# The opening of a one-core encoder layer: keys summed in PSUM in one written order, and a table of delays for the side steps

## The chip, the cores and the metric

The kernel runs on one core of a Trainium2 chip. The metric is the device time of one execution in microseconds (us). Before the change it is 957.74 us, the median of three runs (956.77 to 959.01). About 0.2%, some 2 us, is what a measurement of this kernel can tell from no change.

## The reference, cut to what matters

One transformer-like layer is computed for 512 prompt tokens and 32 sample tokens, together 544 columns. Everything behind it needs `h`, and `h` needs the layer norm of `x` and a shift and a scale that are columns of a matrix product with `w_ada`:

```python
mod = jnp.einsum('bd,de->be', jax.nn.silu(c), w_ada) + b_ada
sh1, sc1, g1, sh2, sc2, g2 = jnp.split(mod[:, None, :], 6, axis=-1)
h = layer_norm(x) * (1 + sc1) + sh1
z = jnp.einsum('btd,de->bte', h, w_in)
a_q, a_k, a_v, m_qk, m_v, m_if, m_o = jnp.split(z, IN_SPLITS, axis=-1)
```

`h` has 1024 features. The first 512 columns of `w_in` give the queries of four attention heads, the next 512 the keys, the next 512 the values. Attention, an mLSTM recurrence with a causal convolution ahead of it, gates, an output projection, two layer norms and a SwiGLU network follow.

## The kernel before

**Arithmetic.** Data are float32. A matmul on TensorE takes the float32r parts of both operands: a tensor is cut into `hi` (a rounded copy, made by ScalarE) and `lo` (the rest, by a subtraction on VectorE or GpSimd), and each product is three matmuls, hi by hi, hi by lo and lo by hi. `h` lies transposed, as eight tiles of 128 features by 544 columns, in `hH` and `hL` (a and b hold tiles 0 to 3 and 4 to 7). The columns are done in two halves, 256 and 288 (`HALF`).

**The stream.** Nearly all work is a list of `Unit`s, run by `stream` (line 678). A unit holds 128 output columns of a weight matrix: for each half it takes a PSUM bank, runs its tiles `k` with three matmuls each (line 604), and evacuates the bank. The weights come through a ring of two 1 MB buffers (`raw_tile`, loaded on SP's queue); the next unit's weights are split while one runs. PSUM has eight banks under four tags: three `g`, two `s`, two `x`, one `o`.

**Side steps.** Transposes, norms, softmax, the recurrence and the outputs are generators. `Lane` (line 34) keeps a reckoned clock while the program is written: `add` queues a generator with a due time, and `run`, called behind each tile `k` of a unit, steps what is due; the due time of the next step is the time so far plus what the generator yields, or the reckoned end of its last instruction (`chain`). So the lane fixes the order of instructions on each engine, not their times. `until` steps everything forward up to a condition. One long generator, `side_all`, holds attention, then four mLSTM heads, then the sample's; it must be through (`need_mn`) before the first unit of `w_br_b`.

**The opening.** The loads go out in order: rows of `x`, and the `w_ada` and `w_in` pieces of five stages of 1, 1, 2, 2 and 2 feature tiles (`STAGES`). For a stage, `ada_gemv` (line 437) makes the shift and scale columns with 32 small matmuls, `ada_first` (line 450) copies them out (`gs`), turns them with transposes (`gt`), reduces and adds the bias (`red`, `modT`), and `modulate` (line 420) makes tiles of `hH` and `hL`. `ORDER0` is a string with one letter for each step of the beginning: transposes of `x`, stage 0, and the first half of its keys and queries (line 507). All else of the queries and keys are units of one stage, one kind and one head, of only one or two tiles `k`. Their partial sums leave PSUM after each stage and are added to `qk` in SBUF by `qk_evac` (line 839): ScalarE writes in stage 0, ScalarE and GpSimd (`qk_t`) or VectorE (line 176) add in the later ones. Every unit takes one `g` bank for each half. `group_split` splits weights with ScalarE and GpSimd (line 157). `start_ada` begins the next stage during the units of one.

**Behind it.** `k_out` (line 866) turns the keys (`k_tok`) and stores them; `q_split` splits the queries. Then come the value units, the gates, convolution units, and so on in the same stream.

Of the kernel before, what the change touches and what calls it, by code (L numbers as in the profile page):

```python
# [32 lines left out]

class Lane:
# [6 lines left out]
    def __init__(self):  # L41
        self.t = 0.0
        self.chain = 0.0
        self.free = {"act": 0.0, "dve": 0.0, "pool": 0.0}
        self.q = []

# [16 lines left out]

    def add(self, gen, delay=0.0):
        item = [max(self.t + delay, self.chain), gen, False]
# [28 lines left out]
def trunk_kernel(ctx: ExitStack, tc: tile.TileContext, I: dict, O: list):  # L94
# [121 lines left out]
    ADA_AT = (0, 0)  # L216
    WARM = 0
    STAGES = (1, 1, 2, 2, 2)
    START = tuple(sum(STAGES[:i]) for i in range(len(STAGES)))
    ada_raw, w_raw = {}, {}  # L220

    def load_ada(s, dst):
        w = STAGES[s] * 128
        if not isinstance(dst, list):
            dst = [dst[:, 8 * i * w:8 * (i + 1) * w] for i in range(2)]
        ada_raw[s] = [d[:, 0:8 * w].rearrange("p (k c) -> p k c", k=8) for d in dst]
        for i in range(2):
            c0 = 1024 * i + START[s] * 128
            load(ada_raw[s][i], w_ada[:, c0:c0 + w].rearrange("(k p) c -> p k c", p=128))

    def load_w(s, dst):
        n = STAGES[s]
        w_raw[s] = dst[:, 0:1024 * n].rearrange("p (i k c) -> p i k c", i=2, k=n)
        for i, c0 in enumerate((512, 0)):
            r0 = START[s] * 128
            load(w_raw[s][:, i], w_in[r0:r0 + n * 128, c0:c0 + 512].rearrange("(k p) c -> p k c", p=128))
# [4 lines left out]
    s2a = [slot(f"2{c}", [128, 2176], F32, f"s2_a{c}") for c in "ab"]  # L241
    s3a = [slot(f"3{c}", [128, 2176], F32, f"s3_a{c}") for c in "ab"]
    s8a = slot(8, [128, 2048], F32, "s8_a")
# [10 lines left out]
    load_ada(0, raw_tile())  # L254
    load_w(0, raw_tile())
# [3 lines left out]
    load_ada(1, s8a)  # L259
    load_w(1, s7a[:, 3072:4096])  # L260
    load_ada(2, s2a)
    load_w(2, s7a[:, 1024:3072])
    load_ada(3, s3a)

# [81 lines left out]
    ORDER0 = "0p0c1c1wwg0gg21grgr2ghrhhh3hr2r3hr3hrammh"  # L346

# [16 lines left out]

    warm = bank("o", "warm")

    def keep_warm(n):
        for _ in range(n):
            tr(warm[:, 0:128], ident, 128)
# [50 lines left out]
    def modulate(k, part=None):  # L420
# [10 lines left out]
        (vtt if part != 0 else gtt)(hL(k)[:, c], t[:, c], hH(k)[:, c].bitcast(F32), SUB)  # L431

    def all_of(gen):
        for _ in gen:
            pass

    def ada_gemv(s):
        n = STAGES[s]
        w = n * 128
        ga = bank("o" if s % 2 else "x", "ga")  # L440
        for i in range(2):
            for k in range(8):
                g = 32 * (k % 4)
                nc.tensor.matmul(
                    ga[g:g + 32, i * w:(i + 1) * w], scT[:, k, :], ada_raw[s][i][:, k, :], start=(k < 4), stop=(k >= 4)
                )
                lane.pe(0.06 * n)
        return ga

    def ada_first(s, ga=None, part=None):  # L450
        n = STAGES[s]
        w = n * 128
        if ga is None:
            ga = ada_gemv(s)
        yield 0
        gs = tmp([128, 512], "gs")
        vcopy(gs[:, 0:2 * w], ga[:, 0:2 * w])
        yield 0
# [3 lines left out]
        yield 0  # L462
# [3 lines left out]
            in_=gt[:, 0:2 * w].rearrange("p (e g c) -> p e c g", g=4, c=32)[:, :, 0:2, :],  # L466
        )
        m = modT[:, 0:16, :].rearrange("p (i k) r -> p i k r", i=2)[:, :, START[s]:START[s] + n, :]
        b = PT[:, c_b_ada:c_b_ada + 16].rearrange("p (i k) -> p i k", i=2)[:, :, START[s]:START[s] + n]
        for i in range(2):  # L470
            vtt(
                m[:, i], red[:, i * n:(i + 1) * n, :], b[:, i].unsqueeze(2).to_broadcast([128, n, 2]), ADD
            )
        yield 0
        ms = [modulate(START[s] + k, part) for k in range(n)]
        for g in ms:
            next(g)
        yield 0
        for g in ms:
            all_of(g)  # L480

    groups = [(s, i) for s in range(len(STAGES)) for i in range(2)]
    parts = {}

    def group_split(x):
        if x in parts or x >= len(groups):
            return
        s, i = groups[x]
        n = STAGES[s]
        r = w_raw[s][:, i]  # L490
        hi = wp.tile([128, 2, 512], F32R, tag="hi", name="hi", bufs=2)
        lo = wp.tile([128, 2, 512], F32R, tag="lo", name="lo", bufs=2)
        act(hi[:, 0:n], r, AF.Copy)
        gtt(lo[:, 0:n], r, hi[:, 0:n].bitcast(F32), SUB)
        parts[x] = (hi, lo)
# [4 lines left out]
    def first_half():  # L500
        for x in range(2):
            hi, lo = parts[x]
            for h in range(4):
                ps = bank("g", "g")
                c = slice(128 * h, 128 * h + 128)
                for p, (w, a) in enumerate(((hi, hH), (hi, hL), (lo, hH))):
                    nc.tensor.matmul(ps[:, 0:256], w[:, 0, c], a(0)[:, 0:256], start=(p == 0), stop=(p == 2))
                act(qk_holder["kq"[x]][:, h, 0:256], ps[:, 0:256], AF.Copy, scale=0.125 if x else 1.0)
                yield

    xg = [x_tile(tt) for tt in range(4)] + [x_rows()]
    pc = silu_c()
    g0 = None
    m1 = None
    fh = first_half()

    def step(c):
        nonlocal g0, m1, ga1
        if c in "0123":
            next(xg[int(c)], None)  # L520
        elif c == "r":
            next(xg[4], None)
        elif c == "c":
            next(pc, None)
        elif c == "g":
            if g0 is None:
                g0 = ada_first(0, ada_gemv(0), 0)
            next(g0, None)
        elif c == "w":
            group_split(len(parts))  # L530
        elif c == "h":
            next(fh, None)
        elif c == "m":
            if m1 is None:
                m1 = modulate(0, 1)
            next(m1, None)
        elif c == "a":
            ga1 = ada_gemv(1)
        elif c == "p":
            load_params(prm_b)  # L540

    ga1 = None
    for c in ORDER0:
        step(c)
    params(prmB, 64)
    load_w(3, raw_tile())
    load_ada(4, slot(6, [128, 4096], F32, "s6_a"))
    load_w(4, raw_tile())
# [17 lines left out]

    def split_w(raw, nk, c0, eng=None):
        r = raw.rearrange("p (k c) -> p k c", c=256)
        hi = wp.tile([128, 8, 128], F32R, tag="hi", name="hi", bufs=2)
        lo = wp.tile([128, 8, 128], F32R, tag="lo", name="lo", bufs=2)  # L570
        act(hi[:, :nk], r[:, :nk, c0:c0 + 128], AF.Copy)
        (eng or vtt)(lo[:, :nk], r[:, :nk, c0:c0 + 128], hi[:, :nk].bitcast(F32), SUB)
        return hi, lo
# [265 lines left out]
    def qk_evac(s, i, h):  # L839
        def f(ps, hf, o, n):  # L840
            dst = qk_holder["kq"[i]][:, h, o:o + n]
            sc = 0.125 if i else 1.0
            if s == 0:
                act(dst, ps[:, 0:n], AF.Copy, scale=sc)
            elif s == 1 and hf:
                t = tmp([128, 288], "qk_t")
                act(t, ps[:, 0:n], AF.Copy, scale=sc)
                gtt(dst, dst, t, ADD)
            else:
                stt(dst, ps[:, 0:n], sc, dst, MUL, ADD)  # L850
                if hf and s == len(STAGES) - 1:
                    if i:
                        q_tasks.append(lane.add(q_split(h)))
                    else:
                        lane.add(k_out(h), 0.5)
# [637 lines left out]
    def stage_part(x, j):  # L1493
        def f():
            group_split(x)
            if j == 1:
                group_split(x + 1)
            c = slice(j * 128, (j + 1) * 128)
            return tuple(t[:, :, c] for t in parts[x])
        return f  # L1500

    fin = {}

    def start_ada(s):
        return lambda: fin.update({s: lane.add(ada_first(s))})

    lane.free = dict.fromkeys(lane.free, lane.t)
    lane.chain = lane.t
    fin[1] = lane.add(ada_first(1, ga1))

    def need_h(s):
        return lambda: lane.until(lambda: fin[s][2])

    for x, (s, i) in enumerate(groups):
        for h in range(4):
            u = Unit(
                None, 0, STAGES[s], hH, hL, qk_evac(s, i, h), ak0=START[s], split=stage_part(x, h),
                halves=(0, 1) if s else (1,),
            )
            if i + h == 0 and s:  # L1520
# [585 lines left out]
```

## Time and profile before

| what | us |
|---|---|
| median of three runs | 957.74 |
| the profiled execution | 960.61 |
| its span, first to last instruction | 958.9 |
| TensorE busy | 915.3 |
| VectorE busy | 524.9 |
| ScalarE busy | 353.5 |
| GpSimd busy | 201.7 |

The profiled execution is 1.7 us longer than its span and 2.9 us above the median. A TensorE row's duration overlaps that of its neighbours, since matmuls are pipelined: the pace is read from the distance of two starts. The granted clock (PEclk) says which share of full speed TensorE was given.

### The profile page before, as it was taken

To read this page: it belongs to the slowest core of one execution; us is meant where nothing else is said; L and a number is where in the kernel's file an instruction comes from. 1 tells how busy PE (TensorE), PEld (TensorE's weight loads), DVE (VectorE), ACT (ScalarE), POOL (GpSimd) and SP (SyncE) were. 2 spreads that over 40 slices of the span, in tenths; PEclk is the share of its full clock that TensorE was granted. 3 is DMA by queue.
4 is the path that set the end of the run, shared out by engine and by line. 5 is a ranking of instruction groups with operands and counts; after the bars stand their busy time and mean duration, and the time that the engine had idled before them with its cause. 6 is when DMAs were issued, how large, how long until landed. Compare 5 with 4: busy or idle time off the path is not lost. (4 is left out here: it accounts for less than half of the span.)

```text
span 958.9 us, 17324 instructions
## 1 busy us (share of the span) xinstructions
PE 915.3 (95%) x7184; PEld 866.9 (90%) x7184; DVE 524.9 (55%) x1124; ACT 353.5 (37%) x686; POOL 201.7 (21%) x241
## 2 busy tenths in 40 slices
PE   5799999999999999999999999999999999999995
PEld 4679998798798989889999989999999999999995
DVE  4657567877554454446855786544444443133257
ACT  4511466455542322322443564322222222122241
POOL 4433016332411110100651665300000000000001
PEclk9989999999999999999999999999999999999998
DMA  9904423252234234242931512022222224532302
GB/s 283 339 2 131 143 67 113 89 175 90 89 116 161 94 118 158 88 139 94 310 97 45 176 50 89 1 89 89 89 89 89 88 89 165 169 101 79 121 2 93
DMA packets 92282, 110.43 MB, mean 115 GB/s; under 512 B 3896, under 2 KB 75660, under 8 KB 92204
## 3 DMA queue, kind: packets, MB, share of 16 engines
q1 hardware_dynamic: 91996, 109.27, 35.2%
q8 instruction: 56, 0.92, 0.4%
q14 instruction: 22, 0.18, 0.1%
q10 hardware_dynamic: 208, 0.07, 0.0%
HBM read 102.09 MB, written 7.24 MB: 114 GB/s over the span
## 5 line engine op out<-in xcount | busy, mean ns | idle before, releaser
L153 DVE TENSOR_TENSOR lo<-raw,hi 128x1024 fp32r<-128x1024 f32 (+3 forms) x102 | 112.0, 1098 | 129.9 <-ACT hi L132 128.6
L132 ACT ACTIVATE hi<-raw 128x1024 fp32r<-128x1024 f32 (+2 forms) x124 | 122.1, 984 | 151.4 <-PE dn L604 61.7
L604 PE MATMUL dn<-act,hi 128*128 128x288 f32 (+1 forms) x704 | 134.8, 290 | 0.0
L604 PE MATMUL g<-hHa,hi 128*128 128x288 f32 (+1 forms) x344 | 109.2, 317 | 6.2 <-DVE qka L176 4.7
L604 PEld LDWEIGHTS dn<-act,hi 128*128 128x128 f32 x704 | 110.0, 188 | 0.0
L604 PE MATMUL g<-hHb,hi 128*128 128x256 f32 (+1 forms) x352 | 107.7, 306 | 1.3 <-DVE qka L176 1.3
L604 PE MATMUL g<-h2Ha,lo 128*128 128x288 f32 (+1 forms) x352 | 101.4, 288 | 2.4 <-POOL lo L157 1.5
L604 PE MATMUL g<-h2La,hi 128*128 128x288 f32 (+1 forms) x352 | 101.4, 288 | 1.0 <-DVE h2La L153 1.0
L604 PE MATMUL g<-h2Ha,hi 128*128 128x288 f32 (+1 forms) x352 | 102.1, 290 | 0.0
L604 PE MATMUL g<-hLa,hi 128*128 128x288 f32 (+1 forms) x344 | 101.2, 294 | 0.7 <-DVE hLa L153 0.6
L604 PE MATMUL g<-hLb,hi 128*128 128x256 f32 (+1 forms) x352 | 101.8, 289 | 0.0
L604 PE MATMUL g<-h2Hb,hi 128*128 128x288 f32 (+1 forms) x352 | 101.7, 289 | 0.0
L604 PE MATMUL g<-h2Lb,hi 128*128 128x288 f32 (+1 forms) x352 | 101.5, 288 | 0.1
L604 PE MATMUL g<-hHb,lo 128*128 128x256 f32 (+1 forms) x352 | 101.5, 288 | 0.0
L604 PE MATMUL dn<-act,lo 128*128 128x288 f32 (+1 forms) x352 | 101.1, 287 | 0.0
L604 PE MATMUL g<-hHa,lo 128*128 128x288 f32 (+1 forms) x344 | 100.9, 293 | 0.2 <-DVE lo L153 0.2
L604 PE MATMUL g<-h2Hb,lo 128*128 128x288 f32 (+1 forms) x352 | 100.9, 287 | 0.0
L157 POOL TENSOR_TENSOR lo<-raw,hi 128x1024 fp32r<-128x1024 f32 (+2 forms) x30 | 63.7, 2123 | 136.5 <-ACT hi L132 126.0
L604 PEld LDWEIGHTS g<-hHa,hi 128*128 128x128 f32 x344 | 66.3, 193 | 23.0 <-issue 6.2
L604 PEld LDWEIGHTS g<-hHb,hi 128*128 128x128 f32 x352 | 66.8, 190 | 5.3 <-issue 2.7
L157 POOL TENSOR_TENSOR rs__10439<-rs__10439,nhalf 128x1 f32<-128x1 f32 x1 | 1.0, 1047 | 325.2 <-DVE rs__10442 L147 325.2
L604 PEld LDWEIGHTS g<-h2Ha,lo 128*128 128x128 f32 x352 | 66.3, 188 | 3.2 <-POOL lo L157 2.0
(480 smaller groups left out, 2163.6 us busy)
## 6 DMA issues: line engine op xcount, KB each, us to landing
raw<-in_w_gu_dram SPq DMA_DIRECT2D x18, 1024.0 KB, 5.1
raw<-in_w_ada_dram SPq DMA_DIRECT2D x16, 1024.0 KB, 5.0
raw<-in_w_in_dram SPq DMA_DIRECT2D x10, 1024.0 KB
raw<-in_w_gate_dram SPq DMA_DIRECT2D x8, 1024.0 KB, 6.7
raw<-in_w_down_dram SPq DMA_DIRECT2D x8, 1024.0 KB, 5.2
wo<-in_w_o_dram SPq DMA_DIRECT2D x4, 1024.0 KB
rawg<-in_w_gu_dram SPq DMA_DIRECT2D x4, 1024.0 KB
raw<-in_w_down_dram SPq DMA_DIRECT2D x3, 768.0 KB
```

The source lines that it names most:

```text
L132: nc.scalar.activation(out=out, in_=in_, func=func, **kw)
L153: nc.vector.tensor_tensor(out=out, in0=in0, in1=in1, op=op)
L157: nc.gpsimd.tensor_tensor(out=out, in0=in0, in1=in1, op=op)
L604: nc.tensor.matmul(ps[:, 0:n], w[:, self.k0 + k, :], a(self.ak0 + k)[:, o:o + n], start=(self.first and k == 0 and p == 0), stop=(self.las ...
```

## The change

- **Stages.** The five stages keep their 1, 1, 2, 2 and 2 tiles. Each loads its `w_ada` columns and only the key half of its rows of `w_in`, one 0.25 MB load for a tile; all go out at the start, into buffers of their own. The first 256 query columns follow as the last load of the opening.
- **Sums in PSUM.** The keys of all four heads are summed over the eight tiles without leaving PSUM: the first halves of four heads in two `g` banks, the second halves in a `g`, two `s` and the `o` bank. ScalarE copies them out once (`e0`, `e1`).
- **One order.** `ORDER` lists all steps up to the keys: `x` for a step of `x`, `g` and `t` for a stage's columns and their turning, `m`, `a`, `b` for the steps of `modulate`, `w` for a split, `A`, `B` for the twelve matmuls of a tile in a half, `q` for the first query split. The `lo` parts of weights and of `h` are made by VectorE, none by GpSimd.
- **Queries.** They are four ordinary units of eight tiles, evacuated by ScalarE.
- **The table.** `LATER` has 114 entries: a name of a generator, which one of its kind, and which step. `Lane.add` and `Lane._step` add the entry, from -3 to 5.4 us, to the reckoned due time. Names of `norm_pair` (22), `attention.block` (21) and `side_all` (33) are the most. In `side_all` the entries for steps 155 to 219 sum to +6.8 us.

```diff
+    def later(self, item):
+        item[4] += 1
+        return LATER.get(f"{item[3]}/{item[4]}", 0.0)
...
-            item[0] = max(self.t + d, self.chain)
+            item[0] = max(self.t + d, self.chain) + self.later(item)
...
+    STAGES = ((0,), (1,), (2, 3), (4, 5), (6, 7))
...
+    ada_at += [slot(i, [128, 2048], F32, f"s{i}_a") for i in ("2a", "2b", "3a", "3b", 8, "5a")]
+    def load_stage(s):
+        load_ada(s, ada_at[2 * s:2 * s + 2])
+        for t in STAGES[s]:
+            load_w(t, w_k[:, t, :])
...
+    def k_split(s):
...
+        act(hi, w_raw[s], AF.Copy)
+        vtt(lo, w_raw[s], hi.bitcast(F32), SUB)
...
+    def acc_open(hf):
+        if hf == 0:
+            for i in range(2):
+                b = bank("g", "k_acc")
+                for j in range(2):
+                    acc[2 * i + j, 0] = b[:, 256 * j:256 * j + 256]
+        else:
+            for h, tag in enumerate("gsso"):
+                acc[h, 1] = bank(tag, "k_acc")[:, 0:288]
...
+        for p in passes:
+            w, a = ((hi, hH), (lo, hH), (hi, hL))[p]
+            nc.tensor.matmul(
+                acc[h, hf], w[:, c], a(s)[:, o:o + n],
...
+    ORDER = (
+        "x1 x0 p c x1 c x0 g0 w0 x2 x1 x2 x4 x0 x4 x3 x4 x2 t0 x4 x4 P a0 x3 g1 o0 t1 a0 x4 x3 A0 x4 b1 b0 o1 b0 a1 b1 a1 g2 w1 B0 t2 A1 m2 m3 B1 m3 w2 m2 g3 w3 B2 A2 t3 m5 B3 A3 m4 w4 m4 m5 g4 w5 B4 t4 m7 m6 m7 A4 m6 A5 w6 B5 A6 B6 w7 A7 q e0 B7 e1"
+    )
...
+            for h in range(NH):
+                act(qk_holder["k"][:, h, HALF[n][0]:sum(HALF[n])], acc[h, n], AF.Copy)
...
+            act(qk_holder["q"][:, h, o:o + n], ps[:, 0:n], AF.Copy, scale=0.125)
...
+    for h in range(NH):
+        lane.add(k_out(h), 1.0 + 2.0 * h)
+    for c in range(2):
+        units += hunits(w_in, c * 256, [q_evac(2 * c), q_evac(2 * c + 1)])
```

More of the change, by code (lines that the diff above doesn't have):

```diff
@@ L45, in __init__ @@
         self.q = []
+        self.count = {}
     def op(self, eng, out, k=1.0):
@@ L258, in trunk_kernel @@
     load_x(3)
[L259 to L263, printed above, removed]
+    for s in range(1, len(STAGES)):
+        load_stage(s)
     make_identity(nc, ident)
@@ L430, in modulate @@
         yield 0
[L431 to L435, printed above, removed]
+        vtt(hL(k)[:, c], t[:, c], hH(k)[:, c].bitcast(F32), SUB)
     def ada_gemv(s):
-        n = STAGES[s]
-        w = n * 128
-        ga = bank("o" if s % 2 else "x", "ga")
+        w = 128 * len(STAGES[s])
+        ga = bank("x", "ga")
         for i in range(2):
@@ L465, in ada_first @@
             out=red[:, 0:2 * n, :], axis=AX.X, op=ADD,
-            in_=gt[:, 0:2 * w].rearrange("p (e g c) -> p e c g", g=4, c=32)[:, :, 0:2, :],
+            in_=gt[:, 0:256 * n].rearrange("p (e g c) -> p e c g", g=4, c=32)[:, :, 0:2, :],
         )
[L468 to L495, printed above, removed]
+        lane.op("dve", red)
@@ L497, in trunk_kernel @@
     qk_holder = {}
     qk_holder["q"], qk_holder["k"] = Halves(5, F32, "qk").h
[L500 to L509, printed above, removed]
+    acc = {}
@@ new lines, in k_mms, with split_w @@
+    def k_mms(s, halves, passes):
+        for hf in halves:
+            for h in range(NH):
+                k_mm(s, h, hf, passes)
+    def split_w(raw, nk, c0, eng=None):
+        r = raw.rearrange("p (k c) -> p k c", c=256)
+        hi = wp.tile([128, 8, 128], F32R, tag="hi", name="hi", bufs=2)
+        lo = wp.tile([128, 8, 128], F32R, tag="lo", name="lo", bufs=2)
+        act(hi[:, :nk], r[:, :nk, c0:c0 + 128], AF.Copy)
+        (eng or vtt)(lo[:, :nk], r[:, :nk, c0:c0 + 128], hi[:, :nk].bitcast(F32), SUB)
+        return hi, lo
@@ L542, in trunk_kernel @@
-    ga1 = None
-    for c in ORDER0:
+        what, n = c[0], int(c[1:] or 0)
+        if what == "x":
+            next(xg[n], None)
+        elif what == "c":
+            next(pc, None)
+        elif what == "p":
+            load_params(prm_b)
+        elif what == "P":
+            params(prmB, 64)
+        elif what == "w":
+            k_split(n)
+        elif what == "g":
+            sums[n] = ada_gemv(n)
+        elif what == "t":
+            ada_turn(n, sums[n])
+        elif what in "mab":
+            part = {"m": None, "a": 0, "b": 1}[what]
+            if (what, n) not in mods:
+                mods[what, n] = modulate(n, part)
+            next(mods[what, n], None)
+        elif what == "o":
+            acc_open(n)
+        elif what in "AB":
+            k_mms(n, ("AB".index(what),), (0, 1, 2))
+        elif what == "e":
+            for h in range(NH):
+                act(qk_holder["k"][:, h, HALF[n][0]:sum(HALF[n])], acc[h, n], AF.Copy)
+        elif what == "q":
+            q_first.append(split_w(q_raw, 8, 0))
@@ L837, in setup, with q_evac @@
             yield 0
-    def qk_evac(s, i, h):
+    def q_evac(h):
         def f(ps, hf, o, n):
[L841 to L855, printed above, removed]
+            act(qk_holder["q"][:, h, o:o + n], ps[:, 0:n], AF.Copy, scale=0.125)
+            if hf:
+                q_tasks.append(lane.add(q_split(h)))
         return f
@@ L1491, in trunk_kernel @@
     SIDE_AT = 3
[L1493 to L1505, printed above, removed]
     lane.free = dict.fromkeys(lane.free, lane.t)
     lane.chain = lane.t
[L1509 to L1520, printed above, removed]
-                u.need = need_h(s)
-            units.append(u)
-            if (i, h) == ADA_AT and 0 < s and s + 1 < len(STAGES):
-                units.append(Call(start_ada(s + 1)))
+    for h in range(NH):
+        lane.add(k_out(h), 1.0 + 2.0 * h)
+    for c in range(2):
+        units += hunits(w_in, c * 256, [q_evac(2 * c), q_evac(2 * c + 1)])
+    q_chunk = units[0].chunk
+    q_chunk.emit = lambda: setattr(q_chunk, 'raw', q_raw)
+    units[0].split = lambda: q_first[0]
     units.append(Call(lambda: lane.add(setup())))
@@ L1537, in trunk_kernel @@
     units += vq
-    vch = [u.chunk for u in units if u.chunk]
-    vch[0].gate = lambda: 7 in parts
-    vch[-1].gate = lambda: 9 in parts
     units.append(IfUnit())
```

225 lines of the change are left out of this document (154 added, 71 removed).

## The prediction

> **What bounds the kernel now.** I read the busy shares first, then busy time by stage, then TensorE's waits, then the order of time at the opening.
>
> ```profile
> span 958.9 us, 17324 instructions
> PE 915.3 (95%) x7184; PEld 866.9 (90%) x7184; DVE 524.9 (55%) x1124; ACT 353.5 (37%) x686; POOL 201.7 (21%) x241
> 0.00:97.60 97.60, 77.65 (x621) 68.80 (x621) 59.92 (x139) 32.86 (x61) 39.24 (x54) 0.93 0.59 186
> 97.60:300.00 202.40, 196.23 (x1531) 176.30 (x1530) 133.75 (x331) 107.53 (x268) 59.30 (x72) 0.99 0.36 113
> 300.00:480.00 180.00, 180.00 (x1391) 164.41 (x1391) 99.74 (x274) 55.56 (x103) 31.32 (x49) 1.00 0.44 146
> 480.00:600.00 120.00, 113.75 (x889) 110.40 (x888) 82.40 (x148) 56.69 (x94) 59.92 (x58) 1.00 0.27 90
> 900.00:959.00 59.00, 47.67 (x377) 47.02 (x375) 33.52 (x60) 16.78 (x25) 4.22 (x4) 0.93 0.19 69
> ```
>
> TensorE is the bound: busy 915.3 of 958.9 us. The stage rows give, in this order, length, then busy time of TensorE, its weight loads, VectorE, ScalarE and GpSimd, then granted clock, DMA share and GB/s. Of 43.6 us of idle TensorE, 20.0 lie in the first 97.6 us, 6.2 in the next stage, 6.3 between 480 and 600, 11.3 at the end. I cut at 97.60 us because there the first value matmul starts (its row stands below), a work item that both kernels have; what lies behind it is a stream that moves forward as a whole if it starts earlier.
>
> In the opening, three more views say what holds it: what the DMA engines moved, TensorE's waits, and the granted clock after a wait.
>
> ```profile
> 0.00:10.00 10.00, 0.34 (x1) 0.18 (x1) 3.23 (x9) 2.83 (x4) 4.34 (x17) 1.00 0.79 239
> 10.00:20.00 10.00, 7.90 (x59) 6.49 (x60) 6.16 (x18) 5.37 (x9) 4.94 (x8) 0.97 1.02 300
> 20.00:30.00 10.00, 10.00 (x95) 9.42 (x93) 5.04 (x18) 7.35 (x20) 2.13 (x5) 0.86 1.08 359
> 30.00:40.00 10.00, 8.42 (x67) 6.54 (x66) 4.51 (x9) 3.84 (x11) 4.82 (x5) 0.83 1.08 359
> PE g L604 <- DVE qka L176: 6.0, 3, 3.5
> PE g L604 <- ACT qka L132: 1.5, 1, 1.5
> 45.38 0.40 PE L604 MATMUL g<-hHa,hi 128*128 128x288 f32 x1 [3.48 <-DVE qka L176]
> 45.00:50.00 5.00, 4.03 (x18) 3.39 (x19) 3.34 (x6) 2.75 (x6) 3.94 (x4) 0.66 0.32 114
> 50.00:55.00 5.00, 5.00 (x45) 3.25 (x44) 1.00 (x3) 0.00 (x0) 1.71 (x1) 0.65 0.00 0
> 55.00:60.00 5.00, 4.99 (x40) 4.79 (x40) 4.12 (x14) 1.90 (x3) 0.00 (x0) 1.00 0.00 0
> ```
>
> The DMA engines are full (share about 1) from 10 to 40 us. TensorE's waits of 6.0 and 1.5 us are for `qka`: a `g` bank whose partial sum had not been added to SBUF yet. After the longest, 3.48 us up to 45.38, the clock was 0.66 and 0.65 for about 10 us. So the opening is held by its data up to about 40 us, and then by evacuations and the clock that they cost.
>
> **Part 1: when the keys are done.** The change doesn't alter the key matmuls, it alters when they can run. By bytes, up to the last key tile there are 2.10 MB of `x`, 0.13 of sample rows, 8.39 of `w_ada` columns and 2.10 of key weights. The query half, 2.10 MB, now comes behind. Stage 3's `w_ada` columns end at 9.57 MB. The rates above sum to 2.39, 5.39 and 8.98 MB at 10, 20 and 30 us, so 9.57 MB have moved at 30 + 0.59/0.359 = 31.6 us, and stage 4's columns (12.19 MB) at 38.9.
>
> A landing is seen by its user somewhat later. The stage-0 query weights end at 2.62 MB, moved at 10.8 us by the same sum, and their split waited for them until 13.26, 2.4 us. So stage 3 is usable at 34.0 and stage 4 at 41.3.
>
> ```profile
> 13.26 0.63 ACT L132 ACTIVATE hi<-raw 128x512 fp32r<-128x512 f32 x1 [1.41 <-DMA raw<-in_w_in_dram]
> 68.80 1.93 PE L444 MATMUL ga<-s_a,scT 128*32 128x256 f32 x32
> 72.28 0.60 PE L142 MATMUL gt<-ident,gs 128*128 128x128 f32 x4
> 72.63 0.37 PE L604 MATMUL g<-hHb,hi 128*128 128x256 f32 x1
> 72.92 0.19 DVE L464 TENSOR_REDUCE red<-gt 128x8 f32<-128x32 f32 x1 [0.34 <-PE gt L142]
> 73.14 0.24 DVE L153 TENSOR_TENSOR modT<-red,PT 128x4 f32<-128x4 f32 x2
> 73.63 1.42 DVE L149 TENSOR_SCALAR mod_t<-xTb,modT 128x512 f32<-128x512 f32 x4
> 61.39 2.67 DVE L153 TENSOR_TENSOR hLb<-mod_t,hHb 128x544 fp32r<-128x544 f32 x2
> L153 DVE TENSOR_TENSOR anb<-qka,ana x4: 681/684/685, 95.2 to 101.1; 128x512 fp32r<-128x512 f32 x4
> 97.60 0.28 PE L604 MATMUL g<-hHa,hi 128*128 128x256 f32 x1
> 100.90 0.29 PE L604 MATMUL g<-hHa,hi 128*128 128x288 f32 x1
> 104.09 0.28 PE L604 MATMUL g<-hHa,hi 128*128 128x256 f32 x1
> 88.03 0.71 PE L142 MATMUL k_tok<-ident,qkb 128*128 128x128 f32 x5
> 88.49 0.38 PE L604 MATMUL g<-hHb,hi 128*128 128x288 f32 x1
> ```
>
> Steps of the written order, at full clock: a stage's 32 column matmuls 1.93 us; its four transposes 0.35 (72.28 to 72.63); the twelve matmuls of a tile in a half. A 288-column half of eight tiles took 3.19 us (100.90 to 104.09), that is 24 matmuls, so twelve take 1.59. The 256-column half took 3.30 from 97.60; 256/288 of 3.19 is 2.84, and the rest is a short wait, so twelve take 1.42.
>
> From 34.0 the order has g3, B2, A2, t3, B3, A3: 1.93 + 2 x (1.59 + 1.42) + 0.35 = 8.3, so g4 starts at 42.3, a little behind its data (41.3): TensorE, not the DMA, sets the end of the keys, by one us. I take it that what comes ahead of g3 fits, since between 26 and 34 us it is g2, t2, A0, B0, A1, B1, 8.3 us. Then g4 1.93, B4 1.59, t4 0.35. Behind t4 VectorE has a chain to tile 6: 0.19 + 0.24 + 1.42 + 2.67 and a weight split of 0.68 (from the 128x512 subtraction), 5.2 us. A4, A5, B5 cover 4.4 of it, and the other 0.8 is a wait. Then A6, B6, A7, B7, 6.0. Sum from 42.3: 1.9 + 1.6 + 0.35 + 5.2 + 6.0 = 15.1, so the keys end at 57.4.
>
> ```profile
> L176 DVE SCALAR_TENSOR_TENSOR qka<-g,qka x28: 402/426/460, 39.9 to 99.0; 128x256 f32<-128x256 f32 x16, 128x288 f32<-128x288 f32 x12
> L132 ACT ACTIVATE qka<-g x8: 384/391/413, 22.0 to 32.5; 128x256 f32<-128x256 f32 x4, 128x288 f32<-128x288 f32 x4
> ```
>
> What the change leaves out, the additions of partial sums, 7.5 us of waits with them, is in this sum already, as there is no bank to wait for; it isn't credited again. VectorE loses these additions (28 of 0.43 for the queries, as many for the keys, 24 us) and gains eight weight splits of 0.68 and stage 0's `lo`, 6 us, so it has room. The two `g` banks of e0 are copied out by four ScalarE copies of 0.39, 1.6 us, under B7's 1.6; without that cover the first query half would wait as long. While the sums are open, only the two `x` banks are left for columns and transposes; a bank is read there by a copy or a reduction before its next use, with matmuls of keys between.
>
> The loads are moved too: in the kernel before, SP's queue held stage 4's loads until tiles of `x` were through, now none of the opening waits for a buffer in use. As the DMA engines were full all the same, I count nothing for that.
>
> **Part 2: queries and the cut.** Four units of eight tiles take 4 x (2.84 + 3.19) = 24.1 us. The query weights end at 13.8 MB, at about 44 us, ahead of their use. Each unit's split (ScalarE, then VectorE) has six us of cover. The keys' transposes cost 0.46 each (88.03 to 88.49), 1.8 for four heads, as before. The first value matmul comes at 57.4 + 24.1 + 1.8 = 83.3.
>
> To this I add a price for the clock. The 10 us at 0.65 above cost about a third of 9 busy us, 3 us. The new order has waits of its own while data come in, and I count half of one such stretch, 1.5: the cut is at 84.8, 12.8 us earlier. Bounds: with no slow clock and landings 2 us earlier 80, which is 17.6 earlier; with two whole slow stretches on the path and DMA 3 us late 92, which is 5.6 earlier.
>
> The Trainium skill ("TensorE: Matmul & The Clock Gate", section "HAM oscillation — how this bites in real kernels") warns against just this form: short bursts of matmuls between waits for data, where each burst starts at half rate; its rule is no idle gap over about 3.4 us. The row at 45.38 agrees with it for one gap of 3.48 us. By that rule the half-rate stretch returns at every stage, and the keys end as the second rival says, not as the sum does.
>
> **Part 3: the table.** It adds and removes no instruction; it reorders them. What it can win is idle time behind the cut, apart from the end, where no entry of the table lies: 6.2 + 6.3 = 12.5 us. Most of its names are in the norm between output projection and network, in attention and in the recurrence, which run in these two stages. It can also lose, or match no step and do nothing: the lists behind the cut are dense, and a later opening state moves every due time even without it. I take 2 us of gain, between 5 of loss and 8 of gain.
>
> **Sum.** 12.8 + 2 = 14.8 us. Against the profiled execution 960.61 - 14.8 = 945.8; that execution stands 2.9 above the median, so the median comes to 957.74 - 14.8 = 943.
>
> **Rivals.**
>
> First, slower: the side chain is late at `need_mn`.
>
> ```profile
> L176 DVE SCALAR_TENSOR_TENSOR mnb<-gg,mn,mna x8: 251/501/752, 319.0 to 455.5; 128x512 fp32r<-128x512 f32 x4, 128x32 fp32r<-128x32 f32 x4
> L604 PE MATMUL g<-mna,hi x64: 278/288/297, 453.5 to 477.2; 128*128 128x256 f32 x32, 128*128 128x288 f32 x32
> 428.10 0.40 PE L136 MATMUL mo_ps<-s_m,mw 32*32 32x129 f32 x2
> ```
>
> The recurrence writes its last `mnb` at 455.5, when the first matmuls that need it have begun (453.5): no slack. The table adds 6.8 us of due time to steps 155 to 219, near the end of that chain. If they run over, the rest stands in front of `w_br_b`'s first unit and TensorE waits through VectorE, ScalarE and GpSimd latencies. The sample's last part, from 428.1 to 455.5, is 27.4 us; all of it in front would make 957.74 - 12.8 + 27.4 = 972. It decides from 12.8 us of overhang on. Against it: the table's own sum is 6.8, and steps that aren't due are pulled forward by the lane, so I give it 4%.
>
> Second, the cold opening: every stage starts at half rate. The stretch from g3 to the keys' end has 20 us of matmuls; half of them at half rate cost 10 us on the path, the cut comes at 93, and with 2 us of the table the time is 951. For it: the clock of 0.83 in 30 to 40 us. Against it: a stage has 8.3 us of work against 7.3 us of data (2.62 MB at 359 GB/s), so the waits should be short and the clock come back. 9%.
>
> Third, nothing: the table loses what the opening wins, or the opening hangs on something not seen here, a landing much later than 41 us or a bank; 957. 3%.
>
> **How the numbers follow.** Forecast, gain of 8 to 22 us: 84%. Cold opening, 951: 9%. Nothing: 3%. Side chain late: 4%. The range goes from the better bounds of both terms, short of their sum (957.74 - 14.8 - 7 = 936), to the cold opening at 951; what lies over that is about one in ten, what lies under it as much. About 0.2%, 2 us, is what can be told from no change; all of the forecast and the cold opening are faster by more. Faster 0.93, same 0.03, slower 0.04.
>
> **What would show it.** Right: the first value matmul (`g<-hHa` in a 256-column half, behind the queries) at about 85 us; no wait of TensorE for `qka`; matmuls of keys behind g4 at about 42; idle TensorE behind the cut about 2 us less than 23.8. Wrong: a granted clock under 0.8 from 40 to 57 us; g4 after 46; TensorE waiting in front of the first matmul on `mna`.

## The result, and the profile after

The changed kernel takes 942.11 us, the median of four runs (940.55 to 942.54); the kernel before took 957.25 us beside it (956.49 to 959.01). The ratio is 0.9836, with a 95% interval of 0.9818 to 0.9855. The profiled execution took 942.38 us. The forecast was 943.0, and its range holds the result, but not for all of the reasons given: with the table taken out, the new opening brings no gain that can be told.

The head of the page of the changed kernel:

```profile
span 940.6 us, 17241 instructions
PE 907.8 (97%) x7184; PEld 864.8 (92%) x7184; DVE 501.2 (53%) x1078; ACT 350.0 (37%) x681; POOL 176.3 (19%) x222
```

TensorE runs the same 7184 matmuls. VectorE has 46 instructions fewer and GpSimd 19 fewer. Next the view by stage, cut at the first value matmul as before (columns as before: length, busy time of TensorE, weight loads, VectorE, ScalarE and GpSimd, then clock, DMA share, GB/s), with the stretch of 30 to 60 us as a last row, and behind it the same stretch of the kernel before:

```profile
0.00:82.90 82.90, 70.07 (x620) 64.71 (x621) 42.55 (x97) 30.33 (x56) 11.97 (x35) 0.98 0.72 219
82.90:285.30 202.40, 198.73 (x1554) 178.86 (x1553) 131.11 (x336) 108.46 (x270) 61.78 (x72) 0.98 0.36 113
285.30:465.30 180.00, 179.88 (x1389) 164.98 (x1388) 100.92 (x268) 55.49 (x104) 33.59 (x52) 1.00 0.46 151
465.30:585.30 120.00, 115.46 (x898) 113.26 (x898) 80.12 (x147) 56.30 (x93) 59.15 (x57) 0.99 0.24 82
885.30:940.60 55.30, 43.66 (x346) 43.03 (x344) 32.79 (x60) 15.94 (x24) 4.22 (x4) 0.94 0.21 74
30.00:60.00 30.00, 30.00 (x274) 27.82 (x274) 18.07 (x40) 11.89 (x23) 1.26 (x4) 1.00 0.62 202
```

```profile
30.00:60.00 30.00, 24.34 (x179) 19.57 (x178) 17.89 (x37) 10.35 (x21) 14.62 (x12) 0.83 0.59 198
```

Four rows of TensorE in order of time (start, duration, engine, line, operation, output and inputs): the columns of stage 4, the last key matmul, the first query matmul, the first value matmul. Behind them, from the view of groups, the first matmuls that need the side chain:

```profile
42.05 1.07 PE L554 MATMUL ga<-s_a,scT 128*32 128x256 f32 x16
56.39 0.30 PE L610 MATMUL k_acc<-hLb,hi 128*128 128x288 f32 x1
56.52 0.27 PE L722 MATMUL g<-hHa,hi 128*128 128x256 f32 x1
82.91 0.28 PE L722 MATMUL g<-hHa,hi 128*128 128x256 f32 x1
```

```profile
L722 PE MATMUL g<-mna,hi x64: 280/288/297, 435.8 to 459.5; 128*128 128x256 f32 x32, 128*128 128x288 f32 x32
```

The span is 18.3 us shorter. Of these, 14.7 come ahead of the cut (97.60 to 82.91), 3.6 behind it: 861.3 us from the cut to the end before, 857.7 after. A second profile of the same instructions, in the last section, splits the gain as 11.7 and 6.2, so each part is good to some 3 us only. About half of the opening's 14.7 is idle time: idle TensorE fell from 20.0 to 12.8 us. Busy TensorE fell from 77.65 to 70.07 us for the same matmuls (621 records, then 620). By the mean clocks, 0.93 and 0.98, slow clock cost an estimated 6.8 us before and 1.7 after, which is 5 of these 7.6 us; the rest isn't split up. The rows of 30 to 60 us show it best: TensorE fully busy at clock 1.00, where the kernel before had 24.34 us of busy time at 0.83. Idle TensorE behind the cut is 20.0 us (3.7, 0.1, 4.5 and 11.6 in the rows above), against 23.8.

### The profile page after: what moved, and what is told of

Same layout as the page of the kernel before. It is cut to its first block, busy times and chain, and to the rows that moved or that the text cites. A ratio compares the mean times of both kernels' runs of the same rounds, so it can differ in the third digit from the quotient of the medians.

```text
span 940.6 us, 17241 instructions
## 1 busy us (share of the span) xinstructions
PE 907.8 (97%) x7184; PEld 864.8 (92%) x7184; DVE 501.2 (53%) x1078; ACT 350.0 (37%) x681; POOL 176.3 (19%) x222
## 4 chain that ended last, share of the span: by engine, by line
PE 80%; DVE 4%; POOL 2%; issue 1%; ACT 0%; DVEq 0%; POOLq 0%
PE g L722 56%; PE dn L722 14%; PE ga L441 2%; PE o_ps L263 1%; PE mo_ps L263 1%; PE qk_ps L263 1%; DVE cv_y L303 1%; PE s_ps L1221 1%; POOL lo L284 1%; PE res_ps L269 1%; PE C_ps L263 1%; DVE lo L280 0%; PE wT_ps L269 0%; PE g L746 0%; DVE y_ta L303 0%
## 5 line engine op out<-in xcount | busy, mean ns | idle before, releaser
L722 PE MATMUL g<-hHa,hi 128*128 128x256 f32 (+1 forms) x320 | 99.4, 311 | 0.0
L722 PE MATMUL g<-hHb,hi 128*128 128x256 f32 (+1 forms) x320 | 97.7, 305 | 0.0
L722 PE MATMUL g<-hLb,hi 128*128 128x256 f32 (+1 forms) x320 | 93.0, 291 | 0.0
L722 PE MATMUL g<-hLa,hi 128*128 128x256 f32 (+1 forms) x320 | 92.7, 290 | 0.0
L722 PE MATMUL g<-hHb,lo 128*128 128x256 f32 (+1 forms) x320 | 92.6, 289 | 0.0
L722 PE MATMUL g<-hHa,lo 128*128 128x256 f32 (+1 forms) x320 | 92.5, 289 | 0.0
L722 PEld LDWEIGHTS g<-hHa,hi 128*128 128x128 f32 x320 | 60.8, 190 | 14.6 <-issue 7.8
L284 POOL TENSOR_TENSOR lo<-raw,hi 128x1024 fp32r<-128x1024 f32 (+1 forms) x24 | 52.5, 2189 | 100.8 <-ACT hi L259 95.0
L722 PEld LDWEIGHTS g<-h2Lb,hi 128*128 128x128 f32 x352 | 66.7, 189 | 0.7 <-DVE h2Lb L280 0.7
L722 PEld LDWEIGHTS g<-h2Hb,lo 128*128 128x128 f32 x352 | 66.8, 190 | 0.0
```

Of the source, the lines that this page charges most:

```text
L284: nc.gpsimd.tensor_tensor(out=out, in0=in0, in1=in1, op=op)
L722: nc.tensor.matmul(ps[:, 0:n], w[:, self.k0 + k, :], a(self.ak0 + k)[:, o:o + n], start=(self.first and k == 0 and p == 0), stop=(self.las ...
```

## The experiments

Each ran beside the kernel before on the same chip; a ratio is to that kernel, with its 95% interval. The median of the kernel before in the three groups of runs was 959.26, 958.72 and 960.14 us. Line numbers are those of each kernel's own file.

**The two halves of the change.** First, the new opening with an empty table:

```diff
-LATER = { ... 114 entries ... }
+LATER = {}
```

> The new opening with an empty table. Theory (the opening brings nearly all, the table 2 us): the first value matmul stays at 82.9 us within 0.3, and the time is 943 to 946 us. Rival, the table is worth nothing: 941.5 to 942.5. Rival, the table brings a good part of the 15 us: 948 or more. Idle TensorE behind the first value matmul tells where: 20.0 us with the table, 22 to 24 expected without.

Measured: 960.21 us, ratio 1.0014 (1.0000 to 1.0028). The theory fell, and by more than the rival asked for. The cut still comes at 82.73 us, but the rest takes 876.0 us, 14.7 more than in the kernel before. The loss is already there in the first 200 us behind the cut. The stage row of this kernel:

```profile
82.73:285.30 202.57, 189.48 (x1453) 169.28 (x1452) 123.54 (x321) 102.67 (x261) 58.10 (x68) 0.96 0.33 106
```

Two places show what went wrong, a first stall at about 135 us and a second at about 205 us. The second is the easier one to read. These are, in order of time, two rows of ScalarE, a load on SP's queue, and ScalarE again; in brackets stands how long an engine sat idle before a row, and what ended that:

```profile
197.93 0.66 ACT L144 ACTIVATE s_g<-s_g 4x544 f32<-4x544 f32 x1 [4.09 <-DVE s_g L165]
200.37 1.04 ACT L144 ACTIVATE hi<-raw 128x1024 fp32r<-128x1024 f32 x1
203.89 0.37 SPq L196 DMA_DIRECT2D raw<-in_w_in_dram  x1
209.29 1.06 ACT L144 ACTIVATE hi<-raw 128x1024 fp32r<-128x1024 f32 x1 [5.98 <-DMA raw<-in_w_in_dram]
```

In about the same stretch of 202 us the changed kernel fits 1554 matmuls, this one 1453. At 197.93 ScalarE has sat idle for 4.09 us ahead of a step of the gates, and in that time it started nothing that stands behind the step. The split of a weight (`hi<-raw`) does stand behind it. So the split is late, GpSimd's `lo` behind it is late (it ends at 203.87), the buffer of the ring comes free late, and the next load is issued late, at 203.89; the next split, at 209.29, waits 5.98 us for that load. What is queued behind that split waits too, among it the copy of softmax weights `wT`, which ends a wait of TensorE of 1.92 us at 210.67. The same rows of the changed kernel:

```profile
195.01 1.06 ACT L259 ACTIVATE hi<-raw 128x1024 fp32r<-128x1024 f32 x1
199.08 0.37 SPq L311 DMA_DIRECT2D raw<-in_w_in_dram  x1
201.69 0.66 ACT L259 ACTIVATE s_g<-s_g 4x544 f32<-4x544 f32 x1 [4.71 <-DVE s_g L280]
204.63 1.06 ACT L259 ACTIVATE hi<-raw 128x1024 fp32r<-128x1024 f32 x1
```

The gates step waits even longer here, 4.71 us, but the split stands ahead of it, the load goes out 4.8 us earlier, and the next split waits for nothing.

The first stall has the longest wait of TensorE behind the cut, and it is the other way round. Without the table, and then in the changed kernel:

```profile
125.08 0.38 SPq L196 DMA_DIRECT2D raw<-in_w_in_dram  x1
131.91 1.06 ACT L144 ACTIVATE hi<-raw 128x1024 fp32r<-128x1024 f32 x1 [3.40 <-DMA raw<-in_w_in_dram]
134.28 0.72 ACT L144 ACTIVATE s_m<-s_m,mx 128x512 f32<-128x512 f32 x1
136.22 1.65 PE L148 MATMUL o_ps<-v_tok,wT 128*128 128x128 f32 x6 [4.78 <-ACT wT L144]
```

```profile
125.75 0.38 SPq L311 DMA_DIRECT2D raw<-in_w_in_dram  x1
129.53 0.62 ACT L259 ACTIVATE s_att<-s_att,mx 128x384 f32<-128x384 f32 x1
131.08 1.05 ACT L259 ACTIVATE hi<-raw 128x1024 fp32r<-128x1024 f32 x1
```

The load is issued as early as in the changed kernel. But without the table ScalarE reaches the split while the load is in flight, waits 3.40 us for it, and the softmax step `s_m` and the `wT` that TensorE needs stand behind the split. In the changed kernel softmax steps (`s_att`) fill that time, and the split then waits for nothing.

Second, the table on the opening of before:

```diff
 # the kernel before, with the table and the lines that read it
+        item[0] += self.later(item)
```

> The kernel before with the table and nothing else. Theory (the table fits the lists behind the new opening, and entries are matched by name and step, so on another state of the lane they fall on other moments): within 3 us of the kernel before, 955 to 960, and the first value matmul at 97.6 within 0.5. Rival, the table is of use by itself: 953 to 955.

Measured: 954.97 us, ratio 0.9951 (0.9930 to 0.9972). The rival's 953 to 955 just holds. The cut came 2.0 us earlier than in the kernel before, not within 0.5 as expected; one profile can't tell 2 us from nothing, as the last section shows. The stages behind this kernel's cut (95.56 us), cut at the same distances:

```profile
95.56:297.96 202.40, 198.69 (x1553) 178.74 (x1552) 133.41 (x340) 109.27 (x271) 61.86 (x72) 0.98 0.36 113
297.96:477.96 180.00, 179.88 (x1389) 164.88 (x1387) 100.72 (x269) 55.36 (x104) 33.64 (x52) 1.00 0.46 152
477.96:597.96 120.00, 115.41 (x897) 113.04 (x896) 80.44 (x147) 56.30 (x93) 59.00 (x57) 0.99 0.24 81
```

Stage by stage these are TensorE's busy times of the changed kernel, within 0.05 us. Behind the cut the two traces have the same 6564 matmuls in the same order: with the table the stream is the same one on either opening, 857.7 us long in both profiles. Without the table the order of these matmuls differs between the openings. And so does the length: 861.3 with the old one, 876.0 with the new. So the gains don't add. The opening alone brings nothing (1.3 us slower, which can hardly be told from no change), the table alone 4.7 us, both together 0.0164 of 957.25, or 15.7 us.

**Parts of the table.** If single stalls cost the time, single entries should give it back. First the three entries of the gates chain alone on the new opening:

```diff
-LATER = {}
+LATER = {"gates_chain/0/11": -1, "gates_chain/0/7": -1, "gates_chain/0/9": 3}
```

> The new opening with only the three entries of the table that move steps of the gates chain (one step pulled forward by 1, one by 1, one put back by 3). The theory now: without the table two stalls cost most of what the opening wins, and the second (TensorE 16.6 of 20 us busy from 200 to 220 us, at a clock of 0.82 and 0.67) begins where ScalarE waits 4.09 us for a gates step with a weight split queued behind it. The three entries move just that step: the second stall should go, about 3.4 us of idle time and some 5 of slow clock, so about 8 us less than without a table: 950 to 954. Rival, many small delays that each give a little: three of 114 entries give almost nothing, 958 to 961. Rival, any other order is as good as the table's: 945 or less.

Measured: 948.65 us, ratio 0.9903 (0.9877 to 0.9929). That is a little better than the theory's 950 to 954, and outside both rivals. Two stretches show what went and what stayed, in the kernel without entries, and in this one:

```profile
130.00:140.00 10.00, 5.22 (x28) 4.97 (x27) 4.75 (x12) 6.83 (x16) 5.75 (x7) 0.73 0.01 4
200.00:220.00 20.00, 16.62 (x96) 14.37 (x96) 9.41 (x29) 8.59 (x23) 5.45 (x8) 0.74 0.24 73
```

```profile
130.00:140.00 10.00, 5.37 (x40) 4.84 (x39) 2.99 (x12) 6.59 (x13) 4.25 (x7) 0.84 0.28 94
200.00:220.00 20.00, 18.41 (x147) 16.29 (x140) 13.74 (x30) 7.91 (x20) 5.36 (x8) 1.00 0.33 106
```

The stall of 200 to 220 us is mostly gone (147 matmuls in place of 96), the one of 130 to 140 is not: there the split still waits 3.25 us, with `s_m` behind it, and TensorE waits 4.63 us.

The table was then cut in two by the time at which its steps run:

```diff
-LATER = { ... 114 entries ... }
+LATER = { ... the 58 entries whose steps run before about 300 us ... }
```

> The new opening with the 58 entries whose steps run before about 300 us (attention, key and query outputs, values, convolution, gates, the remaining columns, the first 155 steps of the side work). Theory: the loss without the table lay from 83 to 285 us, so these entries alone bring nearly all of it back: 942 to 946. Rival, the order behind hangs on the whole table, since each due time follows from those before: 950 or more.

> The new opening with the other 56 entries (the recurrence's state, norms, the second branch's evacuations, steps 155 and up of the side work). Theory: the loss lies ahead of them, so they bring back at most the idle time behind 465 us, about 2 us: 957 to 961. Rival, the two halves of the table are worth about the same: 949 to 953.

Measured: the early 58 entries give 942.89 us, ratio 0.9836 (0.9812 to 0.9859), all of the changed kernel's gain. The late 56 alone give 964.36 us, ratio 1.0060 (1.0043 to 1.0076), worse than no table at all and than both sides had expected: they don't touch the stalls (TensorE busy 5.49 us from 130 to 140, 16.28 from 200 to 220), and add about 4 us. So the early entries carry what the table brings, as the theory said, and no gain of the late ones can be told beside them.

Next the attention and the gates entries together, 25 of them:

```diff
-LATER = { ... 114 entries ... }
+LATER = { ... 21 entries of attention.block, 1 of attention.k_parts, 3 of gates_chain ... }
```

> The new opening with 25 entries: those of attention (22) and of the gates chain (3). Theory: both long stalls of the kernel without a table are weight splits that stand behind side steps in ScalarE's queue; the gates entries removed the second, the attention entries put the softmax steps in front of the first split elsewhere (with the gates entries alone TensorE was busy 5.4 of the 10 us from 130 to 140). Then TensorE is busy 9 us or more there, and the time falls from 948.7 by some 5 us to 942 to 945. Rival, the first stall hangs on other early entries (values, key outputs, the early side steps): 947 to 950, TensorE busy under 7 us from 130 to 140.

Measured: 958.08 us, ratio 0.9983 (0.9968 to 0.9997). This is outside what either side had expected. The same two stretches, and then three rows of ScalarE:

```profile
130.00:140.00 10.00, 5.25 (x44) 4.72 (x42) 1.94 (x9) 5.78 (x12) 3.19 (x2) 0.98 0.31 104
200.00:220.00 20.00, 16.94 (x119) 14.70 (x112) 8.15 (x31) 9.06 (x22) 5.33 (x8) 0.87 0.34 106
```

```profile
201.47 0.66 ACT L170 ACTIVATE s_g<-s_g 4x544 f32<-4x544 f32 x1
203.92 1.04 ACT L170 ACTIVATE hi<-raw 128x1024 fp32r<-128x1024 f32 x1
213.15 1.06 ACT L170 ACTIVATE hi<-raw 128x1024 fp32r<-128x1024 f32 x1 [4.19 <-DMA raw<-in_w_in_dram]
```

The first stall stays: the split at 135.67 waits 4.18 us with `s_m` behind it, and TensorE 4.75 us. The expectation had this stall wrong, since here a split holds up a side step. The second is back, with the gates step again in front of a split; this time the gates step waits for nothing, and ScalarE's wait ahead of it is one of 2.45 us for TensorE at 199.14. An entry does not mend a place by itself: each due time follows from those before it, so with 22 more entries the place that three had mended is late again. Last, another order without any table:

```diff
-    slack = 2.5
+    slack = 3.5
```

> The new opening with an empty table and the lane's slack at 3.5 in place of 2.5 us, so that side steps are emitted while VectorE and ScalarE are planned up to 3.5 us ahead: another order without any table. Theory: the order without a table is one unlucky draw of many, with two long stalls; another draw has other stalls, of 3 to 12 us together behind the cut: 946 to 956. Rival, only a table found for this opening avoids the loss: 958 or more.

Measured: 950.26 us, ratio 0.9910 (0.9885 to 0.9936). The theory held: one number in the lane, with nothing fitted to this opening, brings back 10 us. Here `s_m` runs ahead of the split of the first stall and only `wT` behind it; the split waits 3.61 us, TensorE only 1.85. Of the seven orders tried on the new opening, the one without a table is the second slowest.

In both stalls ScalarE waits for the ring. The table gives the sum of the waits of `hi` for the load of `raw`, between 105 and 240 us, beside the time from the cut to the end, each from one profile.

| kernel | cut, us | cut to end, us | ScalarE waits for the ring, us |
|---|---|---|---|
| changed | 82.9 | 857.7 | 1.8 |
| early entries | 83.2 | 857.7 | 2.4 |
| table on the old opening | 95.6 | 857.7 | 2.5 |
| slack 3.5, no table | 85.5 | 864.7 | 4.0 |
| gates entries | 85.6 | 864.5 | 5.4 |
| before | 97.6 | 861.3 | 8.0 |
| attention and gates entries | 83.7 | 874.9 | 9.2 |
| new opening, no table | 82.7 | 876.0 | 10.8 |
| late entries | 83.7 | 880.1 | 12.4 |

The two columns rise together, but for the kernel before. That speaks for the mechanism and is not proof of it: a split taken off ScalarE's queue, or a third buffer in the ring, was not tried. Which entries mend the first stall stays open as well.

**The opening.** The sums put through SBUF again, with all else as changed: each stage starts its sums anew, ScalarE copies the first, VectorE adds the later ones.

```diff
+    FIRST, LAST = [t[0] for t in STAGES], [t[-1] for t in STAGES]
...
-                start=(s == 0 and p == 0 and (hf == 1 or h % 2 == 0)),
+                start=(s in FIRST and p == 0 and (hf == 1 or h % 2 == 0)),
...
+                    if s == 0:
+                        act(dst, src, AF.Copy)
+                    else:
+                        stt(dst, src, 1.0, dst, MUL, ADD)
```

> The new opening, but the key sums leave PSUM after each stage: ScalarE copies in stage 0, VectorE adds to SBUF in the other four (a bank of two heads at once, so 6 instructions a stage). Same loads, same order, same matmuls. Theory (the sums kept in PSUM are what frees TensorE of waits): some 13 us more of VectorE work in 25 to 56 us, where it is busy 60 to 80%, so the first value matmul comes 3 to 8 us later and the time is 945 to 950. Rival (it is the smaller load ahead of the keys that counts): the first value matmul moves by less than 1 us, 942 to 943.

Measured: 946.58 us, ratio 0.9870 (0.9845 to 0.9895), as the theory expected. That is 0.0034 above the changed kernel's ratio, some 3 us. In its profile the cut comes at 89.22, 6.3 us later than in the changed kernel's and 3.3 later than in the second profile of the same instructions (85.95). VectorE is busy 51.29 us of the first 82.9, against 42.55, and TensorE waits 2.8 us for weight splits that were late (`lo` 1.9, `hi` 0.9). Sums that stay in PSUM are therefore about a fifth of the gain; the greater part comes without them. What the rest of the opening brings, the moved loads and the one order, was not taken apart, but for the place of the query load below.

The key splits' `lo` on GpSimd:

```diff
-        vtt(lo, w_raw[s], hi.bitcast(F32), SUB)
+        gtt(lo, w_raw[s], hi.bitcast(F32), SUB)
```

> The new opening, but the eight lo parts of the key weights are made by GpSimd, as before the change. Theory (it is a small part): GpSimd took 1.28 us for a 128x512 lo where VectorE takes 0.68, so tiles 6 and 7 come up to 1 us later, and VectorE has more time for the rest: first value matmul 0 to 2 us later, 941.5 to 944. Rival (the slow steps of the old opening came from GpSimd and VectorE at work together): 4 us or more, 946 and over.

Measured: 941.19 us, ratio 0.9812 (0.9788 to 0.9836). It can't be told from the changed kernel, and it is a little under the 941.5 that the theory allowed.

Half of the rows of `w_ada` for stages 2 to 4; this kernel leaves out the other half, so it doesn't compute the layer:

```diff
+                load(ada_raw[s][i][:, 0:4, :], w_ada[0:512, c0:c0 + w].rearrange("(k p) c -> p k c", p=128))
+                ada_raw[s][i] = ada_raw[s][i][:, 0:4, :]
```

> The changed kernel, with only the first half of the rows of w_ada loaded for stages 2 to 4 and used twice (leaves out the other half of those rows): 3.15 MB less ahead of the last keys, the instructions on TensorE the same. Prediction's claim, TensorE and not the DMA sets the end of the keys: the last key matmul moves by at most 1.5 us (before 56.4), time 940 to 943. Rival, the stages still wait for their columns: at 0.355 MB/us up to 8.9 us less, time 933 to 938.

Measured: 940.82 us, ratio 0.9812 (0.9787 to 0.9837). The columns of stages 3 and 4, and then the stretch from 40 to 45 us:

```profile
34.58 1.07 PE L558 MATMUL ga<-s3a_a,scT 128*32 128x256 f32 x16
43.10 1.07 PE L558 MATMUL ga<-s_a,scT 128*32 128x256 f32 x16
```

```profile
40.00:45.00 5.00, 5.00 (x59) 3.94 (x57) 3.50 (x9) 2.47 (x4) 0.00 (x0) 1.00 0.00 0
```

The loads are done before 40 us (share 0.00, where the changed kernel has 1.08), and yet g4 is not earlier: 8.52 us behind g3, to the hundredth as in the changed kernel (33.53 and 42.05). The last key matmul starts at 57.44, 1.05 later than in the changed kernel and within the 1.5 expected. TensorE sets the end of the keys.

The query weights ahead of stage 4's columns:

```diff
+        if s == 4:
+            q_raws = [raw_tile(), raw_tile()]
+            q_raw = q_raws[0]
+            for i, t in enumerate(q_raws):
+                load(t.rearrange("p (k c) -> p k c", c=256), w_in[:, 256 * i:256 * i + 256].rearrange("(k p) c -> p k c", p=128))
```

> The changed kernel with the 2.10 MB of query weights loaded ahead of stage 4's columns, so that these land 5.8 us later (2.10 MB at 0.36 MB/us), about 47 us, and TensorE meets one long gap in front of stage 4. By the sum g4 starts at about 47 in place of 42.05 and the first value matmul at 88. With the price of a clock stretch as in the kernel before (a wait of 3.48 us, then 10 us at 0.65, 3 us): first value matmul at 90 to 92, clock 0.6 to 0.8 in the 10 us behind the gap, time 948 to 952. Rival, the gap costs only itself: clock 1.00 behind it, 946 to 948.

Measured: 948.40 us, ratio 0.9884 (0.9861 to 0.9906), the low end of the theory's time; the cut came at 89.0, a little earlier than its 90 to 92. Stage 4's second matrix, and then the stretches around and behind it:

```profile
47.45 1.68 PE L559 MATMUL ga<-s5a_a,scT 128*32 128x256 f32 x16 [1.80 <-DMA s5a_a<-in_w_ada_dram]
```

```profile
45.00:50.00 5.00, 3.20 (x33) 1.60 (x25) 2.46 (x5) 0.27 (x1) 0.00 (x0) 0.78 0.42 145
50.00:55.00 5.00, 5.00 (x38) 5.00 (x38) 3.00 (x9) 1.43 (x3) 0.00 (x0) 0.88 0.02 3
```

The landing at 47.45 is where the sum put it (47). The wait shows as 1.80 us only, since TensorE met the first matrix in time and was itself 2.5 us later than in the profile of the changed kernel. A wait of 1.80 us was followed by a slower clock: 0.78, then 0.88, which cost 1.7 us in all (5 x 0.22 + 5 x 0.12), where 3 were expected. So the gap cost more than itself, and the clock price was about half of the one forecast.

The recurrence's last steps 15 us later:

```diff
-    "side_all/0/212": 3,
+    "side_all/0/212": 18,
```

> The changed kernel with one entry of the table, at step 212 of the side work, raised from 3 to 18 us: the last steps of the recurrence come due 15 us later. The prediction's first rival, made to happen: what is not done when the second branch's first unit is reached is emitted in front of it, and TensorE waits through it. The last four heads' mnb lie from 431.1 to 435.8 in the changed kernel, so at least 4.7 us and, with the steps before them, up to 12 us would stand in front: first matmul on mna at 440 to 448, time 946 to 954. Rival, the lists leave enough room and the steps pulled forward fit beside the first branch: 941 to 944.

Measured: 942.45 us, ratio 0.9824 (0.9799 to 0.9849), and the first matmul on `mna` at 435.9. The order of instructions is the changed kernel's on every engine, row for row. The likely reason, not shown, is that `until` emits step 212: it steps on whatever the due time. So this says nothing on the rival; it is a second profile of the changed program, of use below.

## Why the prediction was right, and where it was not

**Part 1 held.** g4 was put at 42.3 and came at 42.05; the keys' end at 57.4, and it came at 56.5. The claim that TensorE and not the DMA sets it held with half of the columns left out. The start of the sum was right by luck, though: 34.0 was reckoned from the landing of stage 3's columns. g3 came at 33.53, with no wait for a load, and with half of the columns it came no earlier (34.58); in both profiles it follows g2 by 7.81 us, the work that the prediction had put at 8.3 and only took to fit. So TensorE sets the pace from g2 on here, and the reckoned landing happened to fall at the same time. The wait of 0.8 us behind t4 did not come (TensorE is busy throughout from 30 us). Its chain had two `hL` subtractions at 2.67 us, from a row where GpSimd was at work; without it they take 1.44, as the last section shows.

**Part 2 held, with a clock price that is now there and now not.** From the keys' end to the cut 25.9 us were summed and 26.4 measured. A price of 1.5 us was added for slow clock behind the landing of stage 3. From 30 us to the keys' end the clock is 1.00 and nothing was paid; the slow stretch lies ahead of g3. In the changed kernel's profile it cost 1.2 us between 20 and 30 us (clock 0.88; cut at 82.91), in the second profile of the same instructions 4.1 us (0.59; cut at 85.95). Over the eight profiles that share this opening the cut lies between 82.7 and 85.95, 84.2 on average. So 84.8 was a good middle for a wrong place.

**The step that failed is the claim that what lies behind the cut "is a stream that moves forward as a whole if it starts earlier",** and with it Part 3. That part limited the table's gain to the 12.5 us of idle time behind the cut of the kernel before, and took 2 us. Against the kernel before this looks well: 3.6 us behind the cut, or 4.7 by the run of the table alone. But the kernel before was the wrong thing to hold it against. The lane reckons due times from the state in which the opening leaves it, so another opening writes another order; with an empty table that order takes 14.7 us more behind the cut than the old one, the whole gain of the opening. Against that order the table is worth 18 us. Part 3 had a clause that reads "a later opening state moves every due time even without it", and gave it no price. That the two terms could be added, forecast at 12.8 and 2, measured at 14.7 and 3.6, is luck: it holds because this table makes the stream the same on either opening, which the prediction didn't claim. Other tables and settings on the same opening gave 942.89 to 964.36 us.

**The rivals.** The side chain is on time: the last `mnb` (435.8) meets the first matmul on it, and TensorE doesn't wait there. Its own test moved nothing, so it isn't refuted by an experiment. The cold opening did not come: from 30 to 60 us the clock is 1.00 and TensorE never waits 0.3 us. The rule of the Trainium skill ("TensorE: Matmul & The Clock Gate", section "HAM oscillation — how this bites in real kernels"), no idle gap over about 3.4 us, was kept in that stretch; where a gap of 1.80 us was made, the clock fell as in the rows above, at half the gap that the page names. The third rival, "the table loses what the opening wins", at 3%, had the right two terms but the wrong one at fault: it is the order without the table that loses it.

## What to carry to other kernels

- Where a planner or a list of due times writes the order of a long stretch, a gain ahead of it is not carried through by itself: time the earlier part with the later part's order held fixed, and expect other orders to lie many us apart (here 857.7 to 880.1 us for the same work).
- Where an engine starts nothing from behind a step that waits, as ScalarE in these rows, look at what stands behind it, both ways: a weight split behind a late side step delays the next load and the next split, and a side step behind a split whose load is in flight waits for that load.
- Two parts of a change are each to be tried alone: here one alone gave nothing and the other 4.7 us, and both together 15.7.

## What the runs showed of the hardware

**Stretches of slow clock move from one execution of a program to the next.** The changed kernel's profile, and then that of the kernel with step 212 later, which has the same instructions in the same order. The last row of each is the same instruction, with the wait ahead of it:

```profile
20.00:30.00 10.00, 9.21 (x104) 7.08 (x104) 7.19 (x22) 3.40 (x9) 1.21 (x2) 0.88 1.09 353
110.00:115.00 5.00, 5.00 (x29) 4.54 (x26) 2.30 (x14) 1.09 (x5) 0.00 (x0) 0.66 0.01 3
150.00:160.00 10.00, 8.63 (x56) 7.63 (x57) 7.65 (x24) 4.14 (x11) 3.57 (x5) 0.83 0.07 7
109.64 0.39 PE L1221 MATMUL s_ps<-kL,ana 64*128 64x256 f32 x2 [1.24 <-DVE kL L280]
```

```profile
20.00:30.00 10.00, 9.45 (x88) 8.17 (x90) 4.91 (x16) 2.82 (x7) 1.21 (x2) 0.59 1.09 354
110.00:115.00 5.00, 3.76 (x28) 2.96 (x27) 2.96 (x13) 2.31 (x7) 0.04 (x1) 1.00 0.00 0
150.00:160.00 10.00, 8.00 (x64) 6.81 (x63) 9.18 (x25) 4.80 (x12) 5.10 (x6) 1.00 0.04 5
112.69 0.39 PE L1221 MATMUL s_ps<-kL,ana 64*128 64x256 f32 x2 [1.24 <-DVE kL L280]
```

The second loses 4.1 us to the clock from 20 to 30 us and nothing in the other two stretches; the first loses 1.2 us there, and 1.7 in each of the others. Their cuts differ by 3.0 us, and yet the spans are 940.6 and 941.0 us. The same wait of 1.24 us is followed by a slow stretch in one and by none in the other, and so is one of 2.00 us (at 151.37 and 152.94). So a stage time of one profile is good to some 3 us in this kernel, and a cut should not be compared more finely. How long a gap may be without a slow clock, these runs don't show. The Trainium skill ("TensorE: Matmul & The Clock Gate", section "What's actually happening") says that the window over which activity is judged runs freely, so that one kernel has a varying number of slow matmuls at its start. These two profiles agree with it, and show the variation in the middle of a kernel too.

**A VectorE subtraction beside GpSimd can take two to three times as long.** The `hLb` subtractions in the changed kernel, and in the kernel with the key splits' `lo` on GpSimd:

```profile
L280 DVE TENSOR_TENSOR hLb<-mod_t,hHb x4: 718/722/725, 42.8 to 48.8; 128x544 fp32r<-128x544 f32 x4
```

```profile
L280 DVE TENSOR_TENSOR hLb<-mod_t,hHb x4: 726/726/1809, 42.8 to 49.9; 128x544 fp32r<-128x544 f32 x4
```

The one of 1809 ns lies where GpSimd makes a `lo` (43.40 to 46.44); the kernel before had 711 to 2035. The Trainium skill ("SBUF — State Buffer", section "SBUF: two separate sides") states that of two such operations the one that starts first holds a port that both engines share, for its whole length, and the other is blocked. The difference of 1.08 us (1809 less 726 ns), within a GpSimd `lo` of 1.3, agrees. It cost no time that can be told here (941.19 us against 942.11).
